# The down product of a hybrid decoder block: one loop over chunks per Strassen product, in place of groups of chunks

## The chip, the cores and the metric

The kernel runs on one core of a Trainium2 chip. The metric is the device time of one execution in microseconds, the median of three runs. TensorE multiplies, VectorE (DVE), ScalarE (ACT) and GpSimd (POOL) work on elements, SyncE (SP) issues most transfers.

## What is computed

One decoder block on 1024 tokens of width 1024, float32: two token mixers, an output projection, and a feed-forward layer of width 2816. The part that matters here is the end:

```python
u = rmsnorm(h, ln_ffn[l])
h = h + (jax.nn.silu(u @ ffn_w_gate[l]) * (u @ ffn_w_up[l])) @ ffn_w_down[l]
return rmsnorm(h, final_norm)
```

## The kernel before, in words

Every float32 product of the kernel is made of three matmuls (`mm3`, lines 123 to 127): each operand is split into a rounded part (`hi`, made by a cast on ACT) and the rest (`lo`, a subtraction on VectorE or GpSimd), and hi x hi, hi x lo and lo x hi are summed in PSUM. `split_to` (lines 939 to 942) does the cast (line 941) and the subtraction (line 942).

The feed-forward layer cuts each product in two along every dimension and takes seven block products instead of eight (Strassen's scheme in Winograd's form). The gate and up products (lines 1135 to 1149) work through 11 pairs of 128 feature columns; `pair_out` (lines 1039 to 1053) forms the blocks and sums of one pair's activations and stores them to DRAM (`d_a`). For the last pair it is called inside the down stage and its stores are issued by ACT.

The down product contracts over the 2816 features: 11 chunks, each with two row blocks of 128 of the weight matrix `w_d` and its activation blocks from `d_a`. The names of the seven products are those of the activation block and of the weight block or sum: 11 x 11, S2 x T2, 12 x 21, S3 x T3, S1 x T1, 22 x T4 and S4 x 22, with T1 = 12 - 11, T2 = 22 - T1, T3 = 22 - 12, T4 = 21 - T2 of the weight blocks. Each product of one chunk is four token tiles x three matmuls of 128x128 by 128x512.

Before, the 11 chunks stand in five groups (`GROUPS`, line 1156) of 1, 2, 2, 3 and 3. Each group goes through all seven products; `product` (line 1237) loads an activation block per chunk (`load_x`, line 1171), splits it (`unit_split`, line 1193; three of four subtractions on GpSimd) and the weight block (on VectorE), and sums the chunks of the group in four PSUM banks. `add` (line 1251) then adds the banks to SBUF sums `E11` to `E22`, `U2`, `U3`, 24 tiles in all; in the first group the first add of a sum is a copy, every other one on ACT. So each SBUF sum is written once per group. GpSimd also adds the residual (`residual`, line 1184, from `d_h`), and in the last group takes part in the totals (line 1263) and the product with the final gain (line 1273). `finish` (line 1275) does the final norm of a token tile and stores it in two halves. `sums12`, `sum3`, `sum4` (lines 1215 to 1229) make the weight sums on VectorE, in tiles of their own.

Order: the program's order gives each instruction its priority, and a scheduler with a model of the engines fixes the order on every queue when the kernel is built; `ordered_load` (line 895) chains the loads of this stage, so they are issued by SP in program order. Tiles come from pools: `r4` has 14 slots of 128x1024 float32 (`slot`, line 881), which the gate and up stage and the loaded weights share; split operands use eight slots (`wslot`, line 94); activation loads have nine tiles (`xr`). The stage's own pool `dp` lies where the gate and up operands (`T2`, `T3`, `T1`, `B22`) were, so its first tiles wait for the last products of that stage.

Of the kernel before, what the change touches and what calls it, by code (L numbers as in the profile page):

```python
# [20 lines left out]
P = 128  # L21
S = 1024
# [18 lines left out]
# tiles of the second mixer's projection beside each item of the attention, and the loads of their operand  # L41
# [5 lines left out]
def block_kernel(ctx, tc, x, positions, ln_mix, w_in, norm_cq, w_uq, norm_ckv, w_ukv, w_oa,  # L47
# [69 lines left out]
    def wload2(src, n):  # L117
        """two slots, each with half of the contraction; (hi, lo) per chunk of 128"""
        a = wload(src[0:HALF], 4, n)
        b = wload(src[HALF:D], 4, n)  # L120
        return [(w[0][:, c, :], w[1][:, c, :]) for w in (a, b) for c in range(4)]
# [38 lines left out]
    with ExitStack() as s1:  # L160
# [26 lines left out]
        # the first products need the first half of the tokens only  # L187
# [16 lines left out]
    # masks and constants  # L204
# [35 lines left out]
    # decay low-rank and shared rotary key (with its halves also swapped)  # L240
# [25 lines left out]
    # rotary table; rows: cos | signed sin, twice  # L266
# [38 lines left out]
    # log decay (token-major, times 16), its cumulative sum per chunk (feature-major)  # L305
# [25 lines left out]
    # chunked scan, chunk of 128 tokens; within a chunk, pairs of neighbouring blocks of m tokens are  # L331
    # related through the decay at the end of the earlier block, so every exponent is at most zero
# [11 lines left out]
    for half in range(2):  # L344
        for p in range(2):
# [37 lines left out]
            # decays from the chunk start and to the chunk end  # L383
# [56 lines left out]
    # latents and branch gates, kept in DRAM  # L440
# [18 lines left out]
    # output gate of the linear attention  # L459
# [43 lines left out]
    # -1e30 above the diagonal, added to the scores by a product with the identity  # L503
# [18 lines left out]
    def latents(row, n, name):  # L522
        """latents, and the rms factor per token"""
# [18 lines left out]
    def token_rows(rs):  # L542
        """rs[token, tile] along the free axis, on every partition"""
# [10 lines left out]
    # the key and value latents are normed before their products, the query ones through the rotary table  # L554
# [31 lines left out]
    # shared rotary key on every group of 32 rows  # L586
# [16 lines left out]
    # keys and queries: even heads hold [64 plain | 32 rotary | 32 rotary], odd heads [32 | 32 | 64]  # L603
# [44 lines left out]
    # the last gate chunk is cut by token halves, so that the first half of the input makes room early  # L648
# [55 lines left out]
    def values(h, r, pts):  # L704
        acc = ps2.tile([P, 512], F32, name="acc", tag="acc", bufs=1)
        nj = 2 * r + 2
        for j0 in range(0, nj, 2):
            ps = ps2.tile([P, 512], F32, name="pspt", tag="pt", bufs=2)
            # the last pair of key tiles: the second one meets only the second query tile
# [26 lines left out]
    # projection of the second mixer, which fills the end of the attention  # L736
# [36 lines left out]
    def z_first(c, newbank):  # L773
# [5 lines left out]
        for half in range(2):  # L779
            rw = raw[:, half * HALF:(half + 1) * HALF]  # L780
            # softmax denominators, on the rows of their head
# [113 lines left out]
    def ordered_load(dst, src):  # L895
        """a transfer that is issued behind the previous one of this kind"""
        ins = nc.sync.dma_start(dst, src)
        if in_order:
            tc.add_manual_dep(ins.ins, in_order.pop().ins.name,
                              mybir.DependencyInfo(mybir.DependencyClass.NoSync, mybir.DependencyReason.DATA),  # L900
                              reason="issue order")
        in_order.append(ins)
# [36 lines left out]
    def split_to(dst, src, lo_eng=None):  # L939
        """dst[:, 0] + dst[:, 1] = src"""  # L940
# [7 lines left out]
    # The products of the feed-forward layer are cut in two along every dimension and take seven block products  # L948
    # instead of eight (Strassen's scheme in Winograd's form); the sums of blocks are float32, split like any
    # other operand.  # L950
    def wpair(src, fp):
        """the four blocks of two column chunks, and their four sums"""
# [6 lines left out]
    def wsums(w):  # L959
        """S1 = A21 + A22, S2 = S1 - A11, S3 = A21 - A11, S4 = A12 - S2"""  # L960
# [18 lines left out]
    def open_pair(w, e, st):  # L979
        """first block products of a matrix: those that need the first half of the tokens only"""  # L980
# [58 lines left out]
    def pair_out(fp, st):  # L1039
        """blocks of the activations (tokens, features) and their sums for the down product"""  # L1040
# [16 lines left out]
    # the last chunks of the gated sum come last  # L1057
# [16 lines left out]
    # first half of the tokens: blocks B11 and B21; their tiles take T3 and T4 in the end  # L1074
# [27 lines left out]
    def second_half():  # L1102
        """T1 = B12 - B11, T2 = B22 - T1, T3 = B12 - B22 = B11 - T2, T4 = B21 - T2"""
# [51 lines left out]
    fn_b = dp.tile([P, D], F32, name="fn_b")  # L1155
    GROUPS = [[0], [1, 2], [3, 4], [5, 6, 7], [8, 9, 10]]

    def draw():
        return slot("dr")

    E = {}

    def load_down(c):
        b = [draw() if c else dp.tile([P, S], F32, name="d0", tag="tm", bufs=4) for i in range(2)]
        for j in range(2):
            ordered_load(b[j], w_d[0][(2 * c + j) * P:(2 * c + j + 1) * P, :])
        return b

    early = {}

    def load_x(c, nm):
        if (c, nm) in early:
            return early[c, nm]
# [5 lines left out]
    def acc_tiles():  # L1179
        # accumulators per token tile of half 0 and 1 and half of the columns  # L1180
        for nm in ("E11", "E12", "E21", "E22", "U2", "U3"):
            E[nm] = [dp.tile([P, HALF], F32, name=f"E{nm}{t}") for t in range(4)]

    def residual(i, k):
        for t in range(4):
            hr = stg.tile([P, HALF], F32, name="hr", tag="st")
            nc.sync.dma_start(hr, d_h[(4 * i + t) * P:(4 * i + t + 1) * P, k * HALF:(k + 1) * HALF])
            e_ = E[f"E{i + 1}{k + 1}"][t]
            nc.gpsimd.tensor_tensor(e_, e_, hr, ALU.add)

    nsub = list(range(1000))

    def unit_split(x, lo_eng, spare=False):
        t = (slot("us", F32R) if spare else wslot()).rearrange("p (e n) -> p e n", e=2)
        split_to(t, x, lo_eng)
        return t

    # the first loads come before the last sums of the activations
    downs = {}
    for nm in ("11", "S2", "12", "S3", "S1", "22", "S4"):  # L1200
        early[0, nm] = load_x(0, nm)
        if not downs:
            downs[0] = load_down(0)
    parity = 0
    for gi, grp in enumerate(GROUPS):
        lastg = gi == len(GROUPS) - 1
        Y = []
        hv = lambda t: (t[:, 0:HALF], t[:, HALF:S])
        for c in grp:
            b = downs[c]  # L1210
            Y.append(dict(zip(("11", "12", "21", "22"), hv(b[0]) + hv(b[1]))))
        if gi == 0:
            acc_tiles()

        def sums12(n):
            y = Y[n]
# [173 lines left out]
```

## Time and profile before

| | us |
|---|---|
| median of 3 runs (lowest to highest) | 1560.08 (1559.76 to 1561.4) |
| profiled execution, first to last instruction (span) | 1558.8 |
| TensorE busy | 1505.2 (97%) |
| VectorE busy | 945.3 (61%) |
| ScalarE busy | 620.0 (40%) |
| GpSimd busy | 674.5 (43%) |

The span is the only time that is given of the profiled execution; the runs were timed apart from it. Matmuls are pipelined: a matmul's listed duration (about 0.4 us) is longer than the distance from one start to the next, so starts are what to count. Busy shares over the whole span mix stages with different limits; the stage that the change touches is the last 250 us.

### The profile page before, as it was taken

The numbers are of one execution on the slowest core, as the hardware profiler recorded it, in microseconds if no ns is written. First come the engines' busy times: TensorE is split into PE (matmuls) and PEld (weight loads), VectorE is DVE, ScalarE is ACT, GpSimd is POOL, SyncE is SP. The second block draws the span as 40 slices with busy tenths as digits, with TensorE's granted clock in tenths as the row PEclk, the third lists the DMA queues.
The fourth block names the chain that finished last, engine by engine and source line by source line (L and its number), as shares of the span: only waits on it lengthen the run. The fifth ranks groups of instructions, "written<-read, shape, count | busy, mean of one in ns | idle before, by whom it ended". The sixth has DMA issues, their size and how long they took to land.

```text
span 1558.8 us, 20904 instructions
## 1 busy us (share of the span) xinstructions
PE 1505.2 (97%) x7850; PEld 1257.8 (81%) x7850; DVE 945.3 (61%) x1288; ACT 620.0 (40%) x1221; POOL 674.5 (43%) x530
## 2 busy tenths in 40 slices
PE   7999999999999999999999999999999999999996
PEld 6798888898778888887899778888888887787874
DVE  4126676451412766574623866666666666999998
ACT  5335333233423767575313632222222223443444
POOL 4313444423420223234712465555555553466455
PEclk9999999999999999999999999999999999999998
DMA  7211221214411013347622233333333325565312
GB/s 202 58 52 55 68 75 54 75 48 129 128 55 49 9 36 101 102 142 239 242 101 82 95 102 101 102 102 102 102 101 100 100 87 185 196 224 202 108 62 108
DMA packets 123591, 166.87 MB, mean 107 GB/s; under 512 B 12049, under 2 KB 82210, under 8 KB 123490
## 3 DMA queue, kind: packets, MB, share of 16 engines
q1 hardware_dynamic: 122914, 163.70, 32.3%
q10 hardware_dynamic: 576, 1.84, 0.3%
q8 instruction: 62, 1.02, 0.3%
q14 instruction: 39, 0.32, 0.1%
HBM read 117.80 MB, written 47.71 MB: 106 GB/s over the span
## 4 chain that ended last, share of the span: by engine, by line
PE 73%; DVE 11%; issue 6%; POOL 3%; DMA 2%; ACT 2%; POOLq 0%; SPq 0%; DVEq 0%; ACTq 0%
PE ps_mm L126 7%; PE ps_mm L125 7%; PE ps_mm L127 7%; PE psB L126 4%; PE psB L127 4%; PE psB L125 4%; PE psD L125 3%; PE psD L126 3%; PE psD L127 3%; PE psA L125 3%; PE psA L127 3%; PE psA L126 3%; PE acc L722 2%; POOL ws L942 2%; PE pspt L713 2%
## 5 line engine op out<-in xcount | busy, mean ns | idle before, releaser
L125 PE MATMUL ps_mm<-u,wh 128*128 128x512 f32 (+1 forms) x416 | 167.2, 402 | 2.3 <-DVE u L184 1.6
L126 PE MATMUL ps_mm<-u,wh 128*128 128x512 f32 (+1 forms) x416 | 167.2, 403 | 0.0
L127 PE MATMUL ps_mm<-u,wl 128*128 128x512 f32 (+1 forms) x416 | 166.3, 400 | 0.0
L108 POOL TENSOR_TENSOR wl<-wr,wh 128x1024 fp32r<-128x1024 f32 x41 | 101.2, 2475 | 145.4 <-ACT wh L107 126.7
L942 POOL TENSOR_TENSOR ws<-xr,ws 128x512 fp32r<-128x512 f32 x56 | 86.1, 1543 | 67.3 <-ACT ws L941 63.7
L942 POOL TENSOR_TENSOR ws<-sS,ws 128x512 fp32r<-128x512 f32 x44 | 70.6, 1614 | 68.8 <-ACT ws L941 68.8
L125 PEld LDWEIGHTS ps_mm<-u,wh 128*128 128x128 f32 (+1 forms) x416 | 78.2, 188 | 22.9 <-DVE u L184 1.8
L941 ACT CAST ws<-xr 128x512 fp32r<-128x512 f32 x74 | 45.9, 620 | 121.5 <-issue 34.1
L126 PEld LDWEIGHTS ps_mm<-u,wh 128*128 128x128 f32 (+1 forms) x416 | 78.2, 188 | 19.4 <-issue 1.0
L127 PEld LDWEIGHTS ps_mm<-u,wl 128*128 128x128 f32 (+1 forms) x416 | 78.2, 188 | 18.8 <-issue 0.2
L107 ACT CAST wh<-wr 128x1024 fp32r<-128x1024 f32 x41 | 43.0, 1049 | 86.0 <-PE ps_mm L126 24.7
L988 ACT COPY p<-psA 128x512 f32<-128x512 f32 x22 | 12.9, 587 | 157.2 <-PE psA L127 157.2
L125 PE MATMUL ps_mm<-wh,u 128*128 128x256 f32 x256 | 72.3, 282 | 0.0
L127 PE MATMUL ps_mm<-wh,u 128*128 128x256 f32 x256 | 72.2, 282 | 0.0
L126 PE MATMUL ps_mm<-wl,u 128*128 128x256 f32 x256 | 72.2, 282 | 0.0
L126 PE MATMUL psB<-UT,ws 128*128 128x512 f32 x176 | 69.8, 397 | 1.9 <-DVE UT L942 1.9
L125 PE MATMUL psA<-UB,ws 128*128 128x512 f32 x176 | 69.7, 396 | 0.7 <-ACT p L988 0.7
L125 PE MATMUL psB<-UT,ws 128*128 128x512 f32 x176 | 69.7, 396 | 0.1
L127 PE MATMUL psB<-UT,ws 128*128 128x512 f32 x176 | 69.6, 395 | 0.0
L127 PE MATMUL psA<-UB,ws 128*128 128x512 f32 x176 | 69.4, 395 | 0.0
L126 PE MATMUL psA<-UB,ws 128*128 128x512 f32 x176 | 69.3, 394 | 0.0
L126 PE MATMUL psB<-ws 128*128 128x512 f32 x152 | 61.5, 408 | 7.9 <-DVE ws L942 7.9
(429 smaller groups left out, 4563.5 us busy)
## 6 DMA issues: line engine op xcount, KB each, us to landing
xr<-d_a SPq DMA_DIRECT2D x77, 256.0 KB, 3.1
wr<-in_w_in_dram SPq DMA_DIRECT2D x33, 512.0 KB, 3.8
wr<-in_ffn_w_gate_dram SPq DMA_DIRECT2D x22, 512.0 KB, 3.7
wr<-in_ffn_w_up_dram SPq DMA_DIRECT2D x22, 512.0 KB, 3.7
d_a<-p SPq DMA_DIRECT2D x20, 512.0 KB, 2.9
dr<-in_ffn_w_down_dram SPq DMA_DIRECT2D x20, 512.0 KB, 6.4
d_a<-R SPq DMA_DIRECT2D x10, 512.0 KB, 2.6
xt<-in_x_dram SPq DMA_DIRECT2D x8, 512.0 KB, 5.0
```

Of the source, the lines that this page charges most:

```text
L107: nc.scalar.copy(hi, raw)
L108: (lo_eng or nc.gpsimd).tensor_tensor(lo, raw, hi.bitcast(F32), ALU.subtract)
L125: nc.tensor.matmul(ps, ah, bh, start=first, stop=False, **kw)
L126: nc.tensor.matmul(ps, ah, bl, start=False, stop=False, **kw)
L127: nc.tensor.matmul(ps, al, bh, start=False, stop=last, **kw)
L713: nc.tensor.transpose(ps[:, o * P:(o + 1) * P], pts[i][:, (j0 + jj) * P:(j0 + jj + 1) * P], ident)
L722: nc.tensor.matmul(acc[:, a:256], V[j][:, h, :], src[:, jj * 256:jj * 256 + 256 - a], start=j == 0 and k == 0, stop=j == nj - 1 and k == 1 ...
L941: nc.scalar.copy(dst[:, 0], src)
L942: (lo_eng or nc.gpsimd).tensor_tensor(dst[:, 1], src, dst[:, 0].bitcast(F32), ALU.subtract)
L988: nc.scalar.copy(tt[:, 0:HALF], psA)
```

## The change

The five groups are gone. Each of the seven block products now runs over all 11 chunks and sums them in PSUM, and its banks are read once. The order of products is 11, S1 x T1, S2 x T2, S3 x T3, 22 x T4, 12 x 21, S4 x 22. All weight blocks stay in SBUF from the first product on (five first halves and nine second halves in `r4` slots, eight in `dp`), and their sums overwrite them in place. All subtractions, the residual adds and the gain products are on VectorE; GpSimd keeps the sums of the last pair's activations and the power of 128x1 in `rstd_of`. The last pair's `pair_out` is called after the second chunk of the first product. The last three chunks of the last product go token tile by token tile, each tile followed by its `finish`. The diff (its removed lines cut, as the code above shows them; comments that it drops elsewhere are left out):

```diff
         if fp < NPAIR - 1:
             pair_out(fp, st)
 
...
     ux.close()
     dx = ctx.enter_context(ExitStack())
     dp = pool("dp", side="left", c=dx)
...
+    NC = NPAIR
+    IN_R4 = 5
 
     def load_x(c, nm):
...
         i, k = XPOS[nm]
         t = dp.tile([P, HALF], F32, name="xr", tag="xr", bufs=9)
         ordered_load(t, d_a[c][i][:, k * HALF:(k + 1) * HALF])
         return t
 
...
+    halves = lambda t: (t[:, 0:HALF], t[:, HALF:S])
+    Y = [None] * NC
+    Y2 = [None] * NC
+    def load_y(c, j):
+        late = j == 1 and c < NC - 2
+        if (j == 0 and c < IN_R4) or late:
+            t = slot("dr")
+        else:
+            t = dp.tile([P, S], F32, name=f"y{c}{j}")
+        ordered_load(t, w_d[0][(2 * c + j) * P:(2 * c + j + 1) * P, :])
+        (Y, Y2)[j][c] = halves(t)
+    def unit_split(x):
+        t = wslot().rearrange("p (e n) -> p e n", e=2)
+        split_to(t, x, nc.vector)
+        return t
+    def newbanks(k):
+        return [pbank("B", 4) if k else pbank("AD"[t // 2], 2) for t in range(4)]
+    def chunk(ps, c, xname, y, tiles=range(4)):
+        s = unit_split(load_x(c, xname))
+        t = unit_split(y)
+        chunk_mm(ps, c, s, t, tiles)
+        return s, t
+    def chunk_mm(ps, c, s, t, tiles):
+        for i in tiles:
+            ts = slice(i * P, (i + 1) * P)
+            mm3(ps[i], s[:, 0, ts], s[:, 1, ts], t[:, 0], t[:, 1], c == 0, c == NC - 1)
+    def acc(nm):
+        return [dp.tile([P, HALF], F32, name=f"{nm}{t}") for t in range(4)]
+    def plus(dst, a, b):
+        nc.vector.tensor_tensor(dst, a, b, ALU.add)
+    def residual(e, i, k):
         for t in range(4):
...
+            hr = wraw(HALF)
             nc.sync.dma_start(hr, d_h[(4 * i + t) * P:(4 * i + t + 1) * P, k * HALF:(k + 1) * HALF])
...
+            plus(e[t], e[t], hr)
+    ssq = {}
+    def first_half(e, i, k):
+        for t in range(4):
+            ssq[i, t] = small.tile([P, 2], F32, name="ssqf", tag="ssqf", bufs=8)
+            jk = stg.tile([P, HALF], F32, name="jk", tag="st")
+            nc.scalar.activation(jk, e[t], AF.Square, accum_out=ssq[i, t][:, 0:1])
+            nc.vector.tensor_tensor(e[t], e[t], fn_b[:, k * HALF:(k + 1) * HALF], ALU.mult)
+    def finish(done, dst, i, k, t):
+        ks = slice(k * HALF, (k + 1) * HALF)
+        kd = slice((1 - k) * HALF, (2 - k) * HALF)
+        rows = slice((4 * i + t) * P, (4 * i + t + 1) * P)
+        sq, e, d = ssq[i, t], dst[t], done[t]
+        jk = stg.tile([P, HALF], F32, name="jk", tag="st")
+        nc.scalar.activation(jk, e, AF.Square, accum_out=sq[:, 1:2])
+        s1_ = small.tile([P, 1], F32, name="ssq", tag="ssq")
+        plus(s1_, sq[:, 0:1], sq[:, 1:2])
+        r = small.tile([P, 1], F32, name="rx", tag="rx")
+        rstd_of(r, s1_, 1, 1.0 / D, small)
+        nc.scalar.activation(d, d, AF.Copy, scale=r)
+        nc.sync.dma_start(out2[rows, kd], d)
+        nc.vector.scalar_tensor_tensor(e, e, r, fn_b[:, ks], ALU.mult, ALU.mult)
+        nc.sync.dma_start(out2[rows, ks], e)
+    b0 = newbanks(0)
+    for c in range(IN_R4):
+        load_y(c, 0)
+    for c in range(NC):
+        if c + IN_R4 < NC:
+            load_y(c + IN_R4, 0)
+        if c == 1:
+            pair_out(NPAIR - 1, st)
+        if c >= 4:
+            load_y(c - 4, 1)
+        chunk(b0, c, "11", Y[c][0])
+    E11, V5, U2, U3 = (acc(nm) for nm in ("E11", "V5", "U2", "U3"))
+    for t in range(4):
+        nc.scalar.copy(E11[t], b0[t])
+    b1 = newbanks(1)
+    for c in range(NC):
+        if c + NC - 4 < NC:
+            load_y(c + NC - 4, 1)
+        nc.vector.tensor_tensor(Y[c][0], Y[c][1], Y[c][0], ALU.subtract)
+        chunk(b1, c, "S1", Y[c][0])
+    fn_b = dp.tile([P, D], F32, name="fn_b")
+    nc.sync.dma_start(fn_b, final_norm.unsqueeze(0).broadcast_to([P, D]))
+    for t in range(4):
+        nc.scalar.copy(V5[t], b1[t])
+    b0 = newbanks(0)
+    for c in range(NC):
+        nc.vector.tensor_tensor(Y[c][0], Y2[c][1], Y[c][0], ALU.subtract)
+        chunk(b0, c, "S2", Y[c][0])
+    for t in range(4):
+        plus(U2[t], E11[t], b0[t])
+    b1 = newbanks(1)
+    for c in range(NC):
+        nc.vector.tensor_tensor(Y[c][1], Y2[c][1], Y[c][1], ALU.subtract)
+        chunk(b1, c, "S3", Y[c][1])
+    for t in range(4):
+        plus(U3[t], U2[t], b1[t])
+    for t in range(4):
+        plus(U2[t], U2[t], V5[t])
+        plus(V5[t], V5[t], U3[t])
+    E22, E12, E21 = V5, U2, U3
+    b0 = newbanks(0)
+    for c in range(NC):
+        nc.vector.tensor_tensor(Y[c][0], Y2[c][0], Y[c][0], ALU.subtract)
+        chunk(b0, c, "22", Y[c][0])
+        if c == 2:
+            residual(E22, 1, 1)
+        elif c == 5:
+            first_half(E22, 1, 1)
+        elif c == 7:
+            residual(E21, 1, 0)
+    for t in range(4):
+        plus(E21[t], E21[t], b0[t])
+    b1 = newbanks(1)
+    for c in range(NC):
+        chunk(b1, c, "12", Y2[c][0])
+        if c < 4:
+            finish(E22, E21, 1, 0, c)
+        elif c == 6:
+            residual(E11, 0, 0)
+        elif c == 8:
+            residual(E12, 0, 1)
+    for t in range(4):
+        plus(E11[t], E11[t], b1[t])
+    b0 = newbanks(0)
+    LAST = 3
+    for c in range(NC - LAST):
+        chunk(b0, c, "S4", Y2[c][1])
+        if c == 2:
+            first_half(E11, 0, 0)
+    units = [chunk(b0, c, "S4", Y2[c][1], ()) for c in range(NC - LAST, NC)]
+    for i in range(4):
+        for c in range(NC - LAST, NC):
+            chunk_mm(b0, c, *units[c - NC + LAST], [i])
+        plus(E12[i], E12[i], b0[i])
+        finish(E11, E12, 0, 1, i)
```

## Rows read from the trace of the kernel before

**Rows 1.** Busy by stretch: length, PE, PEld, DVE, ACT, POOL, PEclk, DMA share, GB/s
```profile
1250.00:1300.00 50.00, 50.00 (x217) 40.34 (x216) 30.25 (x33) 14.96 (x27) 24.28 (x16) 1.00 0.22 74
1309.20:1546.90 237.70, 223.41 (x925) 178.47 (x924) 231.17 (x302) 104.56 (x197) 136.62 (x92) 0.96 0.46 156
1450.00:1500.00 50.00, 50.00 (x222) 41.09 (x221) 45.84 (x64) 20.91 (x37) 20.09 (x15) 1.00 0.32 100
```

**Rows 2.** Timeline of PE: start us, us, operation, [idle before, releaser]
```profile
1309.00 0.40 PE L127 MATMUL psD<-UB,ws 128*128 128x512 f32 x1
1310.38 0.50 PE L125 MATMUL psA<-ws 128*128 128x512 f32 x1 [0.98 <-ACT ws L941]
...
1320.62 0.39 PE L125 MATMUL psA<-ws 128*128 128x512 f32 x1
...
1503.61 0.39 PE L125 MATMUL psB<-ws 128*128 128x512 f32 x1
...
1511.54 0.39 PE L127 MATMUL psB<-ws 128*128 128x512 f32 x1
...
1516.04 0.50 PE L126 MATMUL psA<-ws 128*128 128x512 f32 x1 [3.20 <-DVE ws L942]
...
1529.26 0.50 PE L126 MATMUL psB<-ws 128*128 128x512 f32 x1 [3.44 <-DVE ws L942]
...
1546.68 0.39 PE L127 MATMUL psD<-us 128*128 128x512 f32 x1
```

**Rows 3.** Groups of instructions, 1309.2 to 1558.8: xcount | busy us, mean ns
```profile
L942 DVE TENSOR_TENSOR ws<-t,ws 128x512 fp32r<-128x512 f32 x44 | 44.1, 1005 | 1.8 <-ACT ws L941 1.7
...
L1256 DVE TENSOR_TENSOR EE<-EE,psB 128x512 f32<-128x512 f32 x40 | 25.6, 674 | 0.8 <-PE psB L127 0.8
...
L942 POOL TENSOR_TENSOR ws<-xr,ws 128x512 fp32r<-128x512 f32 x56 | 86.1, 1543 | 67.3 <-ACT ws L941 63.7 <-issue 1.9 <-DMA dr<-in_ffn_w_down_dram 1.1
L1189 POOL TENSOR_TENSOR EE<-EE,hr 128x512 f32<-128x512 f32 x16 | 25.5, 1603 | 15.5 <-DVE EE L1256 11.5 <-DMA hr<-d_h 4.0
```

**Rows 4.** Timeline of DVE, and of POOL, beside each other from 1503
```profile
1503.33 0.68 DVE L942 TENSOR_TENSOR ws<-xr,ws 128x512 fp32r<-128x512 f32 x1
1503.93 0.68 DVE L942 TENSOR_TENSOR ws<-t,ws 128x512 fp32r<-128x512 f32 x1
1504.54 0.67 DVE L1256 TENSOR_TENSOR EU<-EU,psA 128x512 f32<-128x512 f32 x1
...
1505.73 1.78 DVE L942 TENSOR_TENSOR us<-xr,us 128x512 fp32r<-128x512 f32 x1
...
1505.53 1.44 POOL L942 TENSOR_TENSOR us<-xr,us 128x512 fp32r<-128x512 f32 x1 [3.27 <-ACT us L941]
```

**Rows 5.** Timeline of DVE and SP at the end of the span, 1558.8
```profile
1551.19 0.68 DVE L1256 TENSOR_TENSOR EE<-EE,psD 128x512 f32<-128x512 f32 x1
...
1554.40 0.75 DVE L1290 SCALAR_TENSOR_TENSOR EE<-EE,rx,fn_b 128x512 f32<-128x512 f32 x1 [0.73 <-POOL rx L88]
...
1555.57 0.38 SPq L1291 DMA_DIRECT2D out_dram<-EE  x1
```

**Rows 6.** Timeline of ACT and DVE where the down stage begins
```profile
1308.72 0.35 ACTq L1052 DMA_DIRECT2D d_a<-R  x1
1309.19 0.62 ACT L941 CAST ws<-xr 128x512 fp32r<-128x512 f32 x1 [15.18 <-POOL R L1036]
1309.71 0.61 ACT L941 CAST ws<-d 128x512 fp32r<-128x512 f32 x1
...
1309.43 0.69 DVE L1031 TENSOR_TENSOR UU<-UU,psD 128x512 f32<-128x512 f32 x1 [2.11 <-PE psD L127]
```

**Rows 7.** Busy time by stretch; the page's row of ACT's DMA queue (packets, MB, share)
```profile
1316.00:1332.00 16.00, 16.00 (x66) 13.04 (x65) 16.00 (x24) 11.72 (x23) 5.92 (x5) 0.90 1.02 386
...
q10 hardware_dynamic: 576, 1.84, 0.3%
```

**Rows 8.** Timeline of SP's DMA queue before the stage; its longest wait (us, times, longest)
```profile
1284.12 0.38 SPq L1052 DMA_DIRECT2D d_a<-p  x1
1297.78 0.32 SPq L897 DMA_DIRECT2D xr<-d_a  x1
...
SPq L897 <- PE psB L127: 16.8, 3, 13.2
```

More of the change, by code (lines that the diff above doesn't have):

```diff
@@ L1154, in block_kernel @@
     dp = pool("dp", side="left", c=dx)
[L1155 to L1169, printed above, removed]
+    NC = NPAIR
+    IN_R4 = 5
     def load_x(c, nm):
-        if (c, nm) in early:
-            return early[c, nm]
         i, k = XPOS[nm]
@@ L1177, in load_x @@
         return t
[L1179 to L1184, printed above, removed]
+    halves = lambda t: (t[:, 0:HALF], t[:, HALF:S])
[9 more added lines that the diff above has]
+        (Y, Y2)[j][c] = halves(t)
@@ L1185, in residual @@
+    def acc(nm):
[3 more added lines that the diff above has]
+    def residual(e, i, k):
         for t in range(4):
-            hr = stg.tile([P, HALF], F32, name="hr", tag="st")
+            hr = wraw(HALF)
             nc.sync.dma_start(hr, d_h[(4 * i + t) * P:(4 * i + t + 1) * P, k * HALF:(k + 1) * HALF])
-            e_ = E[f"E{i + 1}{k + 1}"][t]
-            nc.gpsimd.tensor_tensor(e_, e_, hr, ALU.add)
```

157 lines of the change are left out of this document (removed).

## The prediction

> **What bounds the kernel now.** I read the busy time in stretches first, because the change touches one stage only: everything from the last gate and up products to the end. In the stretch before it TensorE is busy all the time and 217 matmuls start in 50 us. In the down stage, 1309.2 to 1546.9, TensorE is busy 223.4 of 237.7 us, but VectorE is busy 231.2 of them, 97%; in the last undisturbed part TensorE again starts 222 matmuls in 50 us at the full granted clock [rows 1]. So the overall line "PE 97%" hides a stage that VectorE sets.
>
> How much TensorE loses there is read from its timeline. At full clock the down matmuls start 0.2266 us apart: 35 pitches between 1503.61 and 1511.54, 7.93 us [rows 2]. The stage has 7 products x 11 chunks x 4 token tiles x 3 matmuls = 924 matmuls, before and after. Their 923 pitches are 209.15 us. Between the first, 1310.38, and the last, 1546.68, lie 236.3 us, so 27.1 us are lost inside. 2.1 of these go in the first 36 matmuls (10.24 us to 1320.62 instead of 8.16). Two of the largest waits are for a VectorE split: 3.20 and 3.44 us [rows 2].
>
> Why VectorE is full is read from its groups. A subtraction of two SBUF operands takes 1005 ns on average in the splits, while an add that reads PSUM takes 674 [rows 3]. The timeline shows the cause: with GpSimd idle three VectorE subtractions and adds follow at 0.60 us; beside a GpSimd operation the same split takes 1.78 us [rows 4]. Each GpSimd operation of that size lasts 1.5 to 1.6 us [rows 3].
>
> **The change, part by part.** *Sums kept in PSUM.* Now each product of a group of 1 to 3 chunks is added to SBUF sums: 28 tile adds in each of four groups and 36 in the last, 148, of which ACT takes 12 copies and VectorE 136 operations like the 674 ns row [rows 3]. Afterwards a product ends once: 20 adds from PSUM on VectorE and 8 copies on ACT (E11, V5).
>
> *GpSimd's work to VectorE.* Moved are 58 splits, 16 residual adds, 8 gain products and 4 totals, 86 operations. VectorE afterwards: 154 splits, 44 sums of weight blocks, 16 residuals, 8 gain products, 8 adds among finished sums, 8 last products, 3 of the last activations, 20 from PSUM: 261. At the clean pitch of 0.605 us (two pitches from 1503.33 to 1504.54, [rows 4]) that is 158 us, beside 209 of TensorE. The work is hidden under the matmuls only if that pitch holds; without it see the third rival.
>
> The same subtraction takes 0.60 us without GpSimd and 1.78 beside it [rows 4], so each operation that leaves GpSimd costs VectorE 0.605 us and frees its neighbour of up to 1.2. The Trainium skill ("Perfetto Trace Analysis", Optimizing Scalar/DVE Operations) warns that work shifted between VectorE and GpSimd may not help, since they share an SBUF port; by that rule the sum would stay near the third rival's 1560. The trace agrees that they block each other, not that the shift is of no use.
>
> *First product.* Each chunk of it needs 12 matmuls, 2.72 us, and only two splits on VectorE, 1.2 us. Before, the first chunk stood for sums and mixed splits. The last gate and up matmul starts at 1309.00, the next could at 1309.23; it came at 1310.38, because ACT's queue stood 15.2 us behind a store of the last activations, which waits for GpSimd [rows 6]. Bounds for the start and the first chunk: 0 (ACT's casts ahead of that store) to 3.2 us (1.15 late, and the 2.08 lost up to 1320.62). I take 2.0, the upper half, as the rows show it, but less, since the chunk's VectorE work is less.
>
> *The last activations' sums and stores* come after the second chunk instead of after 84 matmuls: three VectorE operations, one on GpSimd, four stores on ACT's queue. ACT can stand at such a store again; casts run 0.52 us apart [rows 6], so it has two or three chunks ready by then. Cost from 0 to the same 1.15 us as at the start, included above.
>
> *Loads.* SP's chain now has six loads of down weights, 3.15 MB, ahead of the first activation block, and seven second halves among the rest: 18 x 0.524 + 11 x 0.262 = 12.3 MB in the first product, and the stores of 1.84 MB [rows 7]. At the 386 GB/s seen at 1316 to 1332 [rows 7] these 14.1 MB take 36.6 us. SP issued nothing between 1284.12 and 1297.78 [rows 8], and by then enough of the 14 slots are free for the first five loads (four hold T4, four the last pair's results). Even if all began at 1297.8, the first block would land 8.8 us later, 1306.6, and the last at 1334.4; it is needed at 1309.2 + 10 x 2.72 less 2.2 for casts and splits, 1334.2. So I count 0, with nothing to spare. The other end is the second rival.
>
> *The fifth product* (block 22). In its 132 x 0.2266 = 29.9 us VectorE has 33 splits and sums, 12 adds left by the product before, 8 residual adds and 4 gain products: 57 x 0.605 = 34.5 us. The excess of 4.6 is covered by eight split slots, four chunks of lead, as the product before it needs only 37 x 0.605 = 22.4. Bounds 0 to 4.6; I take 1.0. Residual loads go through SP before activation loads, nine of which are ahead: 0. VectorE could wait for such a load; the same lead covers it. The load of the final gain moves behind the second product on SP and is needed in the fifth: 0.
>
> *Joins of products.* Bounds 0 to 6.6, the two waits for a split [rows 2]; I take 1.0, since splits of the next product don't depend on the sums of the last.
>
> *Tail.* From the start of the last matmul to the add 0.43 us (1309.00 to 1309.43, [rows 2, 6]); from the last add at 1551.19 to the end at 1558.8, 7.6 us [rows 5]: square, root, last product, two stores. The new tail keeps this chain for the last tile; tiles follow by nine matmuls, 2.04 us, while a tile's VectorE work is about 1.4. Now 12.1 us lie between the last matmul and the end, because the adds stand in VectorE's queue; 4.1 are saved.
>
> **Sum.** 1309.23 + 209.15 + 0.43 + 7.6 = 1526.4 us without loss; plus 2.0 + 1.0 + 1.0 = 1530.4. The profiled execution spans 1558.8, 1.3 us under the median of the runs, 1560.08; I keep that distance: **1531.7 us**, 28.4 less. The bounds give 1527.7 to 1542.1.
>
> **Rivals.** *Loads late:* if the slots of the weights come free only when the last pair is done, loading begins at 1309.4 and the eleventh block lands at 1346.0, 11.8 us late: 1543.5. For it: both chains wait on tiles of the stage before, and the first x load waited 13.2 us for TensorE [rows 8]. Against: the count of slots.
>
> *Slower by loads:* the first product goes at the rate of the transfers, and these reach only the stage's mean of 156 GB/s [rows 1], as short loads stand in one chain with long ones. Then 14.1 MB take 90.4 us, the last block lands at 1388.2, 54 late: 1586. It decides below 218 GB/s: with 64.7 us the gain is gone. Against: 386 GB/s over 16 us with the same two sizes of load [rows 7].
>
> *No change:* VectorE stays the bound. If its operations on two SBUF operands stay at 1005 ns for another reason than GpSimd, 241 x 1.005 + 20 x 0.674 = 255.7 us, the stage is as long as it is: about 1560. Against it: the 0.60 us of [rows 4].
>
> **How the numbers follow.** Forecast with its bounds 0.62; loads late 0.20; other losses of 10 to 25 us (an order of queues that the trace of before doesn't show) 0.09; no change 0.03; slower 0.06. A difference of 0.2%, about 3 us, is what a measurement can tell from none. Faster 0.62 + 0.20 + 0.09 = 0.91, same 0.03, slower 0.06. The range 1527 to 1544 holds the bounds and the late loads; 0.18 is left outside.
>
> **What would show it.** Right: VectorE busy about 160 of some 213 us in the down stage, its splits at 0.68 us, matmuls 0.227 apart through nearly every product, the last matmul near 1522, the end about 8 us behind it. Late loads: waits of TensorE or ACT for activation or weight loads before 1345, at half the granted clock. Wrong: VectorE still busy over 90% (GpSimd was not the cause), waits at the joins over 3 us each, a wait of TensorE behind the fifth product, or ACT standing at a store of the last activations while its casts are due.

## The result and the profile after

The changed kernel takes **1541.70 us** (median of 4 runs, 1540.33 to 1543.17), the kernel before 1560.74 (4 runs, 1559.76 to 1562.49): ratio **0.9878 [0.9864, 0.9892]**, 19 us faster. Forecast were 28.4 us and 1531.7; the range 1527 to 1544 holds the result, the sum misses it by 10.

The profiled execution took 1542.38 us and spans 1540.6. Over the span TensorE is busy 1495.2 us (97%), VectorE 879.6 (57%), ScalarE 618.2 (40%), GpSimd 543.1 (35%). Stretches answer to [rows 1]; the columns are length, then busy time with instructions of PE, weight load, VectorE, ACT and GpSimd, then granted clock, DMA share and GB/s:

```profile
1311.30:1532.50 221.20, 213.05 (x925) 175.38 (x924) 161.46 (x264) 102.51 (x194) 7.76 (x9) 0.98 0.48 162
1318.40:1324.50 6.10, 6.10 (x14) 4.77 (x15) 2.55 (x4) 2.20 (x4) 0.00 (x0) 0.50 0.99 299
1324.50:1336.00 11.50, 10.62 (x47) 8.45 (x45) 7.53 (x12) 3.29 (x7) 0.00 (x0) 1.00 1.03 405
1340.00:1360.00 20.00, 20.00 (x90) 16.58 (x89) 18.27 (x30) 11.44 (x22) 0.00 (x0) 1.00 0.72 266
1450.00:1500.00 50.00, 50.00 (x222) 41.40 (x222) 42.87 (x77) 27.91 (x57) 3.04 (x4) 1.00 0.65 212
```

From 1340 on TensorE never stands: 90 matmuls in 20 us, 222 in 50, as in the best stretch of before. VectorE's work in the stage fell from 231 to 161 us. What is lost lies in the first 25 us of the stage. Its groups, against [rows 3]:

```profile
L942 DVE TENSOR_TENSOR ws<-xr,ws 128x512 fp32r<-128x512 f32 x77 | 52.8, 688 | 41.2 <-ACT ws L941 35.8 <-DMA xr<-d_a 5.4
L942 DVE TENSOR_TENSOR ws<-dr,ws 128x512 fp32r<-128x512 f32 x41 | 28.2, 688 | 2.8 <-ACT ws L941 2.8
L1049 DVE TENSOR_TENSOR UU<-R,p 128x512 f32<-128x512 f32 x1 | 1.6, 1632 | 0.0
```

A split takes 688 ns instead of 1005. L1049 still takes 1.63 us: it is the one that runs beside GpSimd's last sum. TensorE's timeline has only two waits left in the stage; against [rows 2]:

```profile
1311.07 0.40 PE L127 MATMUL psD<-UB,ws 128*128 128x512 f32 x1
1318.38 0.79 PE L125 MATMUL psA<-ws 128*128 128x512 f32 x1 [6.92 <-ACT ws L941]
...
1336.35 0.50 PE L125 MATMUL psA<-ws 128*128 128x512 f32 x1 [1.23 <-ACT ws L941]
...
1532.10 0.39 PE L127 MATMUL psD<-ws 128*128 128x512 f32 x1
```

Between the slot after the last gate and up matmul, 1311.30, and the last matmul, 1532.10, lie 220.8 us, 11.65 more than 923 pitches (209.15); before it was 27.1 behind a start that came 1.15 late. The 11.65 are: 7.08 until the first down matmul; 2.97 because the next 14 pitches take 6.14 us, at a granted clock of 0.50 (1.2 GHz) after TensorE had stood for 6.9 us; 1.23 at 1336; and 0.37 in small pieces. So over 11 of 11.65 belong to the first product. What kept ACT is in its timeline (against [rows 6]; ACTq are the transfers that it issues):

```profile
1312.15 0.35 ACTq L1052 DMA_DIRECT2D d_a<-R  x1
1312.62 0.62 ACT L941 CAST ws<-dr 128x512 fp32r<-128x512 f32 x1 [4.79 <-POOL R L1036]
1316.22 1.45 ACTq L1052 DMA_DIRECT2D d_a<-p  x2
1317.71 0.62 ACT L941 CAST ws<-xr 128x512 fp32r<-128x512 f32 x1 [4.47 <-POOL p L1048]
1317.89 0.36 ACTq L1053 DMA_DIRECT2D d_a<-UU  x1
```

The first cast of an activation block (`xr`) starts at 1317.71, behind four weight casts (from 1303.81 on; the last is shown) and three of the four stores. In the program the first chunk's casts come before these stores; in the queue, whose order is fixed when the kernel is built and from modelled times, three of the stores come first. SP's timeline (against [rows 8]) shows that the loads began late too:

```profile
1290.60 8.06 SPq L1207 DMA_DIRECT2D wr<-d_h  x2
1299.08 2.55 SPq L897 DMA_DIRECT2D dr<-in_ffn_w_down_dram  x5
...
1302.80 0.45 SPq L897 DMA_DIRECT2D xr<-d_a  x1
...
1309.69 0.33 SPq L897 DMA_DIRECT2D y<-in_ffn_w_down_dram  x1
1318.00 0.33 SPq L897 DMA_DIRECT2D xr<-d_a  x1
```

Two residual loads that the fifth product needs hold SP from 1290.60 to 1298.66; the first activation load is issued at 1302.80 and lands 8.8 us later, 1311.6. A second gap, 8.3 us from start to start, lies around ACT's stores; the profile names one wait in it, for the landing of ACT's store of `R` (us in all, times, longest):

```profile
SPq L897 <- DMA d_a<-R: 8.0, 1, 8.0
```

The last section shows where this wait comes from. Three theories could explain the lost 11 us: ACT's queue (stores ahead of casts), late loads, or VectorE's queue (sums of the last activations and of the weights ahead of splits).

### The profile page after: what moved, and what is told of

It is laid out like the page before. It is cut to its first block, busy times and chain, and to the rows that moved or that the text cites. A ratio compares the mean times of both kernels' runs of the same rounds, so it can differ in the third digit from the quotient of the medians.

```text
span 1540.6 us, 20721 instructions
## 1 busy us (share of the span) xinstructions
PE 1495.2 (97%) x7850; PEld 1255.6 (82%) x7850; DVE 879.6 (57%) x1250; ACT 618.2 (40%) x1217; POOL 543.1 (35%) x444
## 4 chain that ended last, share of the span: by engine, by line
PE 83%; DVE 6%; POOL 2%; issue 2%; DMA 2%; ACT 2%; DVEq 0%; ACTq 0%; POOLq 0%; SPq 0%
PE ps_mm L126 7%; PE ps_mm L125 7%; PE ps_mm L127 7%; PE psB L126 6%; PE psB L127 6%; PE psB L125 6%; PE psA L125 5%; PE psD L125 5%; PE psD L126 5%; PE psD L127 5%; PE psA L126 4%; PE psA L127 4%; PE acc L722 2%; PE pspt L713 2%; PE pj L125 2%
## 5 line engine op out<-in xcount | busy, mean ns | idle before, releaser
L88 POOL TENSOR_TENSOR rx<-rs_m,nhalf 128x1 f32<-128x1 f32 x24 | 15.1, 637 | 250.8 <-DVE rs_m L87 249.4
L942 DVE TENSOR_TENSOR ws<-xr,ws 128x512 fp32r<-128x512 f32 x77 | 52.8, 688 | 41.2 <-ACT ws L941 35.8
```

What stands on the lines that cost most here:

```text
L88: nc.gpsimd.tensor_tensor(dst, m, nhalf[:, :n], ALU.pow)
L942: (lo_eng or nc.gpsimd).tensor_tensor(dst[:, 1], src, dst[:, 0].bitcast(F32), ALU.subtract)
```

## The experiments

Each edit is made to the changed kernel, except the sixth. Medians stand beside the kernel before in the same session: 1561.26 us in the first (four kernels), 1560.72 in the second (four), 1561.66 in the third (three). A loss is counted from the slot after the last gate and up matmul, in matmul starts against the 0.2266 us pitch; the changed kernel loses 11.6 us in its first 66 matmuls. Theory A of the expectations is the order of the queues, theory B late loads; where they say "after the seventh chunk", the code makes the call ahead of it, after the sixth.

**1. GpSimd issues the last stores.**

```diff
-        put = (nc.scalar if fp == NPAIR - 1 else nc.sync).dma_start
+        put = (nc.gpsimd if fp == NPAIR - 1 else nc.sync).dma_start
```

> Only the four stores of the last pair's activations change: GpSimd issues them instead of ACT. Theory A (after the change, ACT's casts of the first activation blocks stand behind these stores, which wait for a GpSimd sum): the first down matmul starts when its block has landed and is cast, about 1.3 us behind the last gate and up matmul instead of 7.3; 6 us less, and some 2 us less at half clock: 1533 to 1536 us against 1541.7. Theory B (loads late: the first blocks land late behind 3 MB of weights): the wait stays 5 us or more, only named after the load, and later chunks wait too: 1539 to 1542.

Measured: 1541.10 (1538.60 to 1544.19), 0.9872 [0.9857, 0.9887], not told apart from the changed kernel, and above theory A's range. The start wait falls from 6.92 to 1.27 us, and 6 us later a new one stands. TensorE's timeline, then VectorE's:

```profile
1313.48 0.50 PE L125 MATMUL psA<-ws 128*128 128x512 f32 x1 [1.27 <-ACT ws L941]
1319.51 1.22 PE L127 MATMUL psA<-ws 128*128 128x512 f32 x2 [3.89 <-DVE ws L942]
```

```profile
1313.67 2.19 DVE L1256 TENSOR_TENSOR dr<-dr 128x512 f32<-128x512 f32 x1
1315.78 0.68 DVE L1044 TENSOR_TENSOR p<-p,R 128x512 f32<-128x512 f32 x1
1316.49 0.69 DVE L1047 TENSOR_TENSOR p<-p,p 128x512 f32<-128x512 f32 x1
1317.21 1.63 DVE L1049 TENSOR_TENSOR UU<-R,p 128x512 f32<-128x512 f32 x1
1318.77 1.28 DVE L942 TENSOR_TENSOR ws<-xr,ws 128x512 fp32r<-128x512 f32 x2
```

The activation's cast was done at 1313.42, its split starts at 1318.77: a weight sum and three sums of the last pair stand ahead of it. The stores were the first wait in line and not the only one; 8.8 us are lost in the first 66 matmuls. SP issues without the 8.3 us gap here.

**2. The first activation load right behind the first weight load.**

```diff
+    load_y(0, 0)
+    x0 = load_x(0, "11")
-    for c in range(IN_R4):
+    for c in range(1, IN_R4):
         load_y(c, 0)
...
-        chunk(b0, c, "11", Y[c][0])
+        chunk(b0, c, "11", Y[c][0], x=None if c else x0)
```

> Only the order of loads changes: the first activation block is loaded behind the first weight block instead of behind six. Theory A: the first chunk can start near the last gate and up matmul, but the casts of the second chunk still stand behind the stores on ACT's queue until the GpSimd sum is done; most of the wait moves from the first to the second chunk: 1538 to 1541 us. Theory B: the late load was the wait: 6 to 8 us less, 1533 to 1536.

Measured: 1541.37 (1539.85 to 1541.85), 0.9871 [0.9855, 0.9888]. The start wait falls to 0.46; then 3.36 us for a split and 1.28 and 1.23 for casts follow, and 11.2 us are lost in the first 66 matmuls. An earlier load alone moves the wait to the next place in the same queues.

**3. Residual loads chained in program order,** so that SP is free for the weights.

```diff
-            nc.sync.dma_start(hr, d_h[...])
+            ordered_load(hr, d_h[...])
```

> Only the residual loads change: they go into the chain of ordered loads, so that none stands ahead of the weight loads on SP (three did, and SP stood 8 us for tiles at one). The weight loads can begin some 8 us earlier. Theory A: ACT's order is the same, the first down matmul still starts behind the stores, 7 us late: 1540 to 1542 us. Theory B: blocks land 8 us earlier and the wait goes: 1533 to 1536.

Measured: 1544.97 (1543.36 to 1546.15), 0.9895 [0.9880, 0.9910]. The start wait stays 6.92, so the early residual loads do not set it. The late ones cost the fifth product 3.5 us, which neither theory had:

```profile
1451.30 0.50 PE L125 MATMUL psA<-ws 128*128 128x512 f32 x1 [3.14 <-ACT ws L941]
```

**4. The three edits together.**

> The three edits together: stores issued by GpSimd, the first activation block ahead, residual loads in the chain. Both theories: the first down matmul follows the last gate and up matmul with under 1 us of wait, no half clock, tail as it is: 1530 to 1533 us. Theory A alone: no better than 2 us over the stores alone. Theory B alone: some 6 us better than the stores alone.

Measured: 1545.59 (1544.86 to 1546.86), 0.9901 [0.9886, 0.9916], a miss. The start wait is gone, but waits of 1.71, 1.23, 2.15 and 1.23 us follow (9.1 lost in the first 66 matmuls), and the fifth product loses 6.7. That is twice as much as in the third experiment mostly because of the clock. There the wait was 3.14 us and the granted clock stayed at 1.00; here it is 3.50 us, and the next 14 pitches run at half clock, 2.97 us more. The stretches behind the two waits, third experiment first (columns as in the result):

```profile
1451.30:1454.30 3.00, 3.00 (x13) 2.36 (x14) 3.00 (x7) 2.49 (x6) 0.00 (x0) 1.00 0.97 337
1450.50:1456.90 6.40, 6.36 (x15) 4.99 (x16) 6.24 (x11) 3.82 (x9) 0.00 (x0) 0.52 0.66 225
```

**5. The last pair's sums and stores ahead of the seventh chunk,** not of the second.

```diff
-        if c == 1:
+        if c == 6:
             pair_out(NPAIR - 1, st)
```

> Only the place of the last pair's sums and stores changes: after the seventh chunk of the first product instead of after the second. Theory A, widened by the run with GpSimd's stores (there the wait went from ACT's queue to VectorE's, 3.9 us behind the same sums): the sums and stores stand ahead of the first activation splits in both queues. Then TensorE waits under 2 us before the first down matmul, loses 3 to 5 us in the first 66 matmuls instead of 11, and the time is 1534 to 1537 us against 1541.7. Theory B (loads late): the waits stay, behind the loads of the first blocks: 1539 to 1542.

Measured: 1538.74 (1537.94 to 1539.51), 0.9861 [0.9844, 0.9877], between the ranges of the two theories; 5.9 lost in the first 66. With the sums out of both queues' first places 3 us come back. A start wait of 2.35 remains: the store of `R` is still ahead of the casts on ACT, and SP still stands from 1309.39 to 1317.74.

**6. The kernel before, without GpSimd:** its 86 operations go to VectorE.

```diff
-                units.append((unit_split(load_x(grp[n], a), nc.gpsimd if nsub.pop() % 4 else nc.vector, by_tile),
+                units.append((unit_split(load_x(grp[n], a), nc.vector, by_tile),
...
-            nc.gpsimd.tensor_tensor(e_, e_, hr, ALU.add)
+            nc.vector.tensor_tensor(e_, e_, hr, ALU.add)
...
-            total("E22", "U3", nc.gpsimd)
+            total("E22", "U3", nc.vector)
```

(the gain product in the same way)

> The kernel before with one part of the change alone: its 86 GpSimd operations of the down stage go to VectorE, the groups and their adds stay. Theory of the prediction: VectorE has some 388 operations at 0.605 us, 235 us, as long as the contended 231 of before; its splits fall to 0.69 us, it stays busy over 95%, and the time stays at 1555 to 1566 us. Rival (GpSimd's neighbourhood was the whole loss): 1540 to 1546, as the changed kernel.

Measured: 1556.39 (1554.99 to 1557.76, 6 runs), 0.9971 [0.9960, 0.9983]. Its stage and its splits:

```profile
1309.20:1546.00 236.80, 220.91 (x936) 174.58 (x934) 232.78 (x399) 106.45 (x202) 6.97 (x8) 0.99 0.49 163
```

```profile
L942 DVE TENSOR_TENSOR ws<-xr,ws 128x512 fp32r<-128x512 f32 x74 | 50.1, 677 | 1.6 <-ACT ws L941 1.6
```

The splits fall to 677 ns as read, but VectorE now has 399 instructions and is busy 232.8 of 236.8 us: a faster operation and more of them. In this trace 8.5 fewer us are lost between the matmuls of the stage (19.8 instead of 28.3, start included), but from the last matmul to the end are 14.2 us instead of 12.1. Alone this half is worth 4 us.

**7. The changed kernel with three of four activation splits on GpSimd.**

```diff
-        s = unit_split(load_x(c, xname))
+        s = unit_split(load_x(c, xname), nc.gpsimd if nsub.pop() % 4 else nc.vector)
```

> The changed kernel with the other part undone: three of four splits of activation blocks are on GpSimd again, as before. Theory of the prediction: VectorE has some 203 operations; where GpSimd works beside it, those on two SBUF operands go to about 1.0 us, 196 us in all, still less than TensorE's 209; the time rises by 0 to 6 us to 1542 to 1548. Rival (the sums in PSUM bring nothing by themselves): 1555 or more.

Measured: 1549.60 (1548.19 to 1550.66), 0.9928 [0.9913, 0.9943], 11 us under before and 1.6 over the range forecast. VectorE's weight splits are back at 1053 ns; the start is as in the changed kernel (7.08), and between the middle of the fifth product and that of the sixth 7.8 us are lost, the largest wait 3.02 us:

```profile
L942 DVE TENSOR_TENSOR ws<-dr,ws 128x512 fp32r<-128x512 f32 x41 | 43.0, 1053 | 16.1 <-ACT ws L941 16.1
```

```profile
1474.92 0.53 PE L126 MATMUL psA<-ws 128*128 128x512 f32 x1 [3.02 <-DVE ws L942]
```

So all of the change but the 58 splits is worth 11 of the 19 us: the sums in PSUM, the new tail (8.4 us instead of 12.1 here) and the 28 other operations moved off GpSimd, which no run takes apart. The splits off GpSimd are worth another 8 us where the sums are gone; the whole move was worth 4 without that. The intervals (about 3 us on the 8 and 2 on the 4) do not quite part the two.

**8. Sums ahead of the seventh chunk, stores by GpSimd, and the first three activation loads each behind its weight load.**

```diff
     for c in range(IN_R4):
         load_y(c, 0)
+        if c < 3:
+            xs.append(load_x(c, "11"))
```

(the other two edits as in 5 and 1)

> Three edits for the start: the last pair's sums and stores after the seventh chunk, the stores issued by GpSimd, and the first three activation blocks loaded each behind its own weight block. Nothing of the last pair and no late block stands ahead of the first three chunks. Theory A and B: the first down matmul waits under 0.6 us, the first 66 matmuls lose under 3 us: 1531 to 1534 us. If it stays over 1538, the cause of the start is neither.

Measured: 1539.87 (1539.27 to 1542.11), 0.9869 [0.9854, 0.9884], a miss. The first matmul comes without a wait; then 1.23, 3.15 and twice 1.23 us, and 6.6 are lost in the first 66 matmuls. TensorE, then ACT, then VectorE:

```profile
1319.50 0.50 PE L125 MATMUL psA<-ws 128*128 128x512 f32 x1 [1.23 <-ACT ws L941]
1324.76 0.73 PE L127 MATMUL psA<-ws 128*128 128x512 f32 x2 [3.15 <-DVE ws L942]
```

```profile
1318.31 0.62 ACT L941 CAST ws<-y 128x512 fp32r<-128x512 f32 x1 [2.10 <-PE psD L127]
1318.84 0.61 ACT L941 CAST ws<-xr 128x512 fp32r<-128x512 f32 x1
```

```profile
1320.53 1.78 DVE L1047 TENSOR_TENSOR p<-p,p 128x512 f32<-128x512 f32 x1
...
1324.03 0.68 DVE L942 TENSOR_TENSOR ws<-xr,ws 128x512 fp32r<-128x512 f32 x1
```

At 1319.50 the cast of the activation that TensorE waits for stands behind the cast of a later weight, and that one waits until TensorE gives back a split slot: TensorE is kept waiting by work that waits for TensorE. The slots are no lead if the queue fills them with weights first. At 1324.76 it waits for the split of the same activation. Its cast was done at 1319.45, and the split came on VectorE at 1324.03, behind the last pair's three sums, two weight sums and a weight split.

**9. Casts and splits of the first product kept in program order, nothing else.** (Instructions so marked keep their order among each other; one of the last pair's sums, L1044, was marked already.)

```diff
-        split_to(t, x, nc.vector)
+        if pin:
+            tc.keep_in_program_order(nc.scalar.copy(t[:, 0], x))
+            tc.keep_in_program_order(nc.vector.tensor_tensor(t[:, 1], x, t[:, 0].bitcast(F32), ALU.subtract))
+        else:
+            split_to(t, x, nc.vector)
...
-        chunk(b0, c, "11", Y[c][0])
+        chunk(b0, c, "11", Y[c][0], pin=True)
```

> The pinned order of the first product's casts and subtractions alone; the last pair's work still stands after the second chunk. Theory A: the waits of chunks behind weight casts go (1.2 us at 1336 and the lost lead); the start improves only where activation casts had stood behind later weights; the second chunk still waits for the last pair's sums: 5 to 8 us lost in the first product instead of 11, 1536 to 1540 us. Theory B: no change, 1541 to 1543.

Measured: 1550.65 (1548.17 to 1551.52), 0.9929 [0.9915, 0.9944], worse than the changed kernel and outside both ranges. Now the queue is nearly the program's: the store of `R`, the first chunk's casts, the other three stores, the second chunk's casts. TensorE, ACT, and the last sum that a `p` store needs, on VectorE:

```profile
1329.87 1.22 PE L125 MATMUL psA<-ws 128*128 128x512 f32 x2 [14.65 <-ACT ws L1182]
```

```profile
1309.36 0.35 ACTq L1052 DMA_DIRECT2D d_a<-R  x1
1309.82 0.62 ACT L1182 CAST ws<-xr 128x512 fp32r<-128x512 f32 x1 [15.18 <-DMA xr<-d_a]
1310.35 0.61 ACT L1182 CAST ws<-dr 128x512 fp32r<-128x512 f32 x1
1323.21 2.97 ACTq L1052 DMA_DIRECT2D d_a<-p  x2
1328.23 0.33 ACTq L1053 DMA_DIRECT2D d_a<-UU  x1
1328.67 0.62 ACT L1182 CAST ws<-xr 128x512 fp32r<-128x512 f32 x1 [17.71 <-DMA dr<-in_ffn_w_down_dram]
```

```profile
1314.18 1.77 DVE L1047 TENSOR_TENSOR p<-p,p 128x512 f32<-128x512 f32 x1
```

The data of both `p` stores were ready by 1315.95 (GpSimd's sum ended at 1315.40), yet ACT issues the first at 1323.21. The releaser printed for the cast at 1328.67 names a weight load, though the cast reads an activation block: ahead of it on ACT stood the stores, and the chain that ended last goes through them to that load. From `R`'s store to the cast at 1328.67 it is, with the pieces between left out:

```profile
1309.36 6.74 DMA d_a<-R
1316.11 0.33 SPq L897
...
1319.77 8.38 DMA dr<-in_ffn_w_down_dram
```

So SP waits until ACT's store has landed, and ACT's last store, issued at 1328.23, waits until a load of SP has landed.

**10. The same with the sums ahead of the seventh chunk and the stores by GpSimd** (edits of 5 and 1).

> As the run with the four edits, but with the loads in the order of the changed kernel: six weight blocks ahead of the first activation block. Theory A: one wait of 1 to 2 us for the first block's landing, then none; 2 to 4 us lost in the first product; 1533 to 1535 us. Theory B: the first block and later ones are waited for, 6 us or more lost, 1537 to 1541.

Measured: 1537.05 (1536.30 to 1538.89), 0.9847 [0.9832, 0.9861]. The time lies at the lower end of theory B's range, but 4.3 us are lost in the first 66 matmuls, not 6, and 6.8 in all; waits of 1.36 (the first activation's landing), 0.71 and two of 0.60.

**11. And each activation load of the first product but the last right behind its weight load.**

```diff
     for c in range(IN_R4):
         load_y(c, 0)
+        xs[c] = load_x(c, "11")
...
             load_y(c + IN_R4, 0)
+            if c + IN_R4 < NC - 1:
+                xs[c + IN_R4] = load_x(c + IN_R4, "11")
```

> Four edits: the casts and split subtractions of the first product are pinned to the program's order on ACT and VectorE (activation, weight, chunk by chunk), the last pair's sums and stores come after the seventh chunk, GpSimd issues the stores, and each activation block but the last is loaded behind its own weight block. Theory A, as it now stands (what costs is what stands ahead in ACT's and VectorE's queues: the last pair's work, and weight splits that wait for one of eight slots ahead of activation splits): no wait over 0.5 us in the first product, under 1.5 us lost in it, 1531 to 1533 us. Theory B (transfers can't keep up with the first product): TensorE still waits there 5 us or more, behind loads, 1536 to 1540.

Measured: **1534.54** (1534.05 to 1535.65), **0.9829 [0.9813, 0.9846]**, the fastest of all: 7 us under the changed kernel, and 1.5 over theory A's range. Its span is 1533.0; its timeline of TensorE:

```profile
1311.03 0.40 PE L127 MATMUL psD<-UB,ws 128*128 128x512 f32 x1
1311.27 0.62 PE L125 MATMUL psA<-ws 128*128 128x512 f32 x2
...
1314.48 0.50 PE L126 MATMUL psA<-ws 128*128 128x512 f32 x1 [1.76 <-DVE ws L1183]
...
1524.50 0.39 PE L127 MATMUL psD<-ws 128*128 128x512 f32 x1
```

The down product starts with no gap, the granted clock stays at 1.00, and 1524.50 - 1311.26 - 209.15 = 4.1 us are lost in all, half of them at the wait of 1.76 us for a split, where theory A had none over 0.5. The difference to the tenth, 2.5 us, is the price of the late activation loads; the 4 to 5 between the changed kernel and the tenth belong to three edits together, the pinned order, the place of the sums and the issuer of the stores.

## Why the prediction was right, and where it was wrong

**VectorE as the bound, and GpSimd as what slows it: right.** Splits at 688 ns, VectorE 161 of 221 us, no wait of TensorE after 1336.35. VectorE's 158 us were forecast, the matmul pitch and the count of 923 hold. The mechanism has two halves: the sixth experiment gives 4 us for the move alone, the seventh 11 for the changed kernel with 58 splits back on GpSimd, both together 19. That they help each other is likely but not shown: the 4 us by which 19 exceeds the sum of the two are about the noise of three such differences (some 2 us each). The Trainium skill ("Perfetto Trace Analysis", Optimizing Scalar/DVE Operations) warns that shifting work between VectorE and GpSimd may not help. The sixth experiment shows that it does, by 0.29%, and also how near the warning comes: VectorE stays busy 98% of the stage until the sums go as well.

**Joins and the fifth product: 0, where 1.0 each was taken.** The bounds held. But the fifth product is free only because its residual loads were issued early; chained, they cost 3.5 us (third experiment). The sentence that the lead would cover a late residual load did not hold there.

**First product: the step that failed.** Taken were 2.0 us within 0 to 3.2; measured are 7.08 + 2.97 + 1.23, about 11.3. The prediction wrote of ACT that "casts run 0.52 us apart [rows 6], so it has two or three chunks ready by then". Two things are wrong in that. It places the call of `pair_out` after the second chunk, as the description of the change does too; the code calls it at `c == 1` ahead of the second chunk's products, so after the first, and one chunk can be ready by then. And it takes the program's order for that of the queues: ACT had three stores and four weight casts ahead of the first activation cast, VectorE the last pair's sums ahead of the first activation split. The bound of 3.2 came from the start of before, where 84 matmuls lay between the start and those sums, and that start was misread: up to 1320.62 only 24 matmuls start, not 36, so 4.80 us were lost there and not 2.08, and the bound would have been 5.95, still half of what came. Further, for a store that comes earlier the nearest row was the 15.2 us that ACT had stood at the first of them [rows 6]. ACT standing at a store while its casts are due was named as what would show the forecast wrong, at no price beyond 1.15 us. Nor did the sum hold a term of its own for the half clock after a long wait (2.97 us here).

**Loads: counted as 0, partly wrong.** SP was not free from 1284.12 to 1297.78, since residual loads moved into that gap; weights began at 1299.08 and the first activations landed at 1311.6 instead of by 1306.6. By the tenth and eleventh experiments that is worth about 2.5 us; in the changed kernel most of it hides behind ACT's queue (an earlier first load alone gained nothing in the second experiment). The rate was right: 405 GB/s between 1324.5 and 1336.

**Tail and the rest.** From the last matmul to the end are 8.5 us, forecast 8.03. The last gate and up matmul came at 1311.07 instead of 1309.00, though TensorE's order up to there is the same; in the other profiles it lies between 1309.6 and 1311.8. By TensorE's 5200th matmul the 2 us are there already (906.45 us before, 908.53 after), 400 us ahead of the stage; over all 13 profiles the place varies from 1309.00 to 1311.81, so it is no effect of the change that these runs can show. The account of the span: 1530.4 + 2.1 (upstream) + 7.65 (11.65 instead of 4.0) + 0.5 (tail) = 1540.6.

**The rivals.** Of the late loads the time was nearly right (1543.5), for another reason; what came is the mechanism of the case with 0.09, "an order of queues that the trace of before doesn't show", at a loss near its lower end of 10 us. The range held the time by luck: its upper part was there for the late loads. Slower and no change did not come.

## What to carry to other kernels

Where a scheduler fixes the order of in-order queues when the kernel is built, a stage's start is costed from the queues that can reach it and not from the program's order: write down for each engine what may stand ahead of the first instruction that the bound engine waits for, stores and slot waits included. Removing the first such wait shows the next (experiments 1, 2, 4 and 8); it took the order of the casts, the place of the sums, the issuer of the stores and the order of the loads together to get 7 us, and the order of the casts alone cost 9. Where transfers of two queues take their semaphores from one set, as SP's and ACT's do here, a store also waits for loads and a load for stores. Two halves of a change that relieve the same engine are to be run apart: here 4 and 11 us, and 19 together.

## What the runs showed that was not expected

A store issued by ACT while SP's loads run can hold ACT far beyond its data: in the ninth experiment 7.3 us after both `p` tiles were ready (1315.95 to 1323.21), in which ACT ran nothing. SP has a gap of 8.3 us around ACT's stores in the changed kernel (1309.69 to 1318.00), 8.35 in the fifth experiment and 8.35 in the ninth; in each of the three the profile names one wait of 8.0 us, for the landing of `R`'s store. The traces show why. The landings of SP's and ACT's transfers are signalled on the same eight semaphores, used nearly in turn, and a transfer starts only when the one that had its semaphore before has landed: of some 125 such transfers after 1250 us, in the changed kernel and in the ninth experiment alike, none starts earlier. In the ninth, ACT's three late stores start at 1323.21, 1325.85 and 1328.23; the loads of SP that had their semaphores before landed at 1323.13, 1325.77 and 1328.15. `R`'s store landed at 1316.10, and SP's next load starts at 1316.11. So the two queues wait for each other through the program's semaphores. The stores that GpSimd issued (first, tenth, eleventh) have four semaphores of their own, and no gap of SP as long is there. The kernel before has such a wait too, 7.2 us of SP for `R`'s store, which the prediction did not price.

After a wait of 6.9 us TensorE ran 14 pitches at 0.43 us, at a granted clock of 0.50, before it came back to 0.227: 3 us on top of the wait. After the wait of 3.89 us in the first experiment seven pitches took 3.15 us, instead of 1.59; after 6.92 us in the third and 14.65 us in the ninth only six pitches were that long. In the eleventh, after 1.76 us, only the first was longer (0.34), and the granted clock of that stretch is 1.00:

```profile
1314.00:1316.00 2.00, 1.52 (x7) 1.26 (x8) 1.97 (x4) 0.00 (x0) 0.00 (x0) 1.00 1.02 328
```

What decides is left open, and the length of the wait alone does not: what followed waits of 3 us and more lay between nothing (3.14 us, the fifth product of the third experiment) and 3.0 us (3.50 us, that of the fourth).
